# Hybrid decoder block on one core: which stage prepares the stored low parts of the later projection weights

## The chip, the cores and the metric

The kernel runs on one core of a Trainium2 chip. The metric is the device time of one execution in microseconds (us); the median of three runs is given. All data is float32. TensorE computes the matmuls, VectorE (DVE), ScalarE (ACT) and GpSimd (POOL) work between them, and SyncE (SP) issues almost all DMAs. Each engine executes its instructions in the order in which they stand in its queue.

## The reference

One decoder block for a sequence of 1024 tokens with 1024 channels, batch 1. Two branches work on the same normalized input h: attention with 16 heads in stick-breaking form, and a pooling branch.

```python
h = rms_norm(x, norm_gain) * (1 + scale) + shift
q, k, v, z_a, u, z_b, m_a, m_b = split(h @ w_in)          # eight times 1024 columns
p_a = (attention(q, k, v) * silu(z_a)) @ w_branch_a
pooled = (window_mean(u) - u) @ pool_w * pool_scale       # per group of 256 channels, windows 2, 4, 8, 16
p_b = (pooled * silu(z_b)) @ w_branch_b
merged = sigmoid(m_a) * p_a + sigmoid(m_b) * p_b
out = rms_norm(x + gate * (merged @ w_out), final_gain)   # shift, scale, gate = split(silu(c) @ w_ada + b_ada)
```

## The kernel before

**Three matmuls for one.** Every operand of a large product is kept as two tiles: a high part (a cast to a reduced float32 format, `fp32r` in the profile, on ScalarE) and a low part (the operand minus its high part, on VectorE or GpSimd). A product is then high·high + high·low + low·high. So each weight that TensorE uses must first be loaded, cast and subtracted.

**Stages.** In order: the modulation vectors and h (tile `hT`), with the u projection, whose weights are multiplied with `pool_w` first; the *values' stage*, v = h·W_v in two halves of eight tiles (`v{sb}_{hf}`, lines 600 to 627); the *gate's stage*, eight tiles of z_b = h·W (`wzb0` to `wzb7`, lines 662 to 687), each followed by a silu and a multiplication with the pooled differences `d0` to `d7`, written to `gb`; the *products* (lines 750 to 778), p_b = gb·w_branch_b in seven products p1, p5, p6, p7, p4, p3, p2 (a Strassen-Winograd scheme), each with 48 matmuls in two halves q; then 40 weight tiles of *projections* (k, q, z_a and the gates m_a, m_b) with the attention woven in, in a pinned order; then the output.

**The products' banks.** Four banks of PSUM hold the sum of the chain p1, p6, p7, p4. Each of these products adds into what the one before has left there, so ScalarE copies the four banks out in between (`s1` after p1, `s2` after p6, `s3` after p7, `s4` after p4, line 743). The operands of each half are cast into `p1a0`, `p1b0` and so on: the weights (`a`) into two buffers of the pool `wts` (tag `whl`), which the weights of the gate's stage use too; the data (`b`) into three buffers (tag `bhl`).

**Stored low parts.** The order of the 40 projection tiles is in `tiles`. For the first `PLAIN` = 8 of them `load_parts` loads the weight, casts it and subtracts (on GpSimd, tile `MASKED` on VectorE) just ahead of use. For the other 32 the low part is made much earlier, by `make_lo` (lines 147 to 165): load the weight into `l{i}_raw`, cast it into `l{i}_hi` on ScalarE, subtract in place on VectorE, and store the result to `wl_d` in memory; `load_parts` then loads it from there. How many are made where is set by three rows of numbers: eight after the u tiles, `LO_V` after each tile of the values (in each half), `LO_ZB` after each weight of the gate's stage, `LO_PB` after each product. Each call takes buffers from the pool that it is given: three for `l_raw`, one for `l_hi`.

**Buffers.** A tile's buffer is reused when the last reader is done; for `l_raw` this is the store to `wl_d`. In the gate's stage the rows of `w_gate` (`wg0` to `wg7`, the gate vector is summed from them on VectorE, line 686) share the three `lraw` buffers of the pool `pb`. The pool `dif` holds the window sums and differences at the far end of the memory; it is closed after the gate's stage, and `sums` is opened there.

**Order.** The program is written stage by stage, but outside of pinned parts a scheduler puts each engine's queue in order by its own estimate of time. The queues of the built program are shown below where the change moves them.

Of the kernel before, what the change touches and what calls it, by code (L numbers as in the profile page):

```python
# [9 lines left out]
F32 = mybir.dt.float32  # L10
# [5 lines left out]
P = 128  # L16
D = 1024
# [16 lines left out]
NWT = 4  # L34


PLAIN = 8

MASKED = 4
LO_V = (1, 0, 1, 1, 0, 1, 1, 0)  # L40
LO_ZB = (0, 1, 0, 1, 0, 1, 0, 1)
LO_PB = (1, 2, 1, 2, 1, 2, 1)

DIFFS = {1: 0, 4: 1, 7: 2, 10: 3}
HD = 64
# [12 lines left out]
def block_kernel(ctx, tc, a, out):  # L58
# [3 lines left out]
    def pool(name, **kw):  # L62
        return tc.tile_pool(name=name, bufs=1, reuse_waits="tile", **kw)
# [9 lines left out]
    def bank(tag, name):  # L73
        return psp.tile([P, 512], F32, tag=tag, bufs=BANKS[tag], name=name)
# [59 lines left out]
    def load_w(src, name, hi_eng, lo_eng):  # L134
        raw = wts.tile([P, KB, P], F32, tag="raw", bufs=2, name=name + "_raw")
        nc.sync.dma_start(raw.rearrange("p k c -> p (k c)"), src)
        return split(raw, [P, KB, P], wts, "whl", 2, hi_eng, lo_eng, name)
# [6 lines left out]
    tiles += gates  # L144
    early_lo = iter(range(PLAIN, len(tiles)))

    def make_lo(pl, n, bufs=3, later=False):

        rest = []
        for _ in range(n):  # L150
            i = next(early_lo)
            raw = pl.tile([P, D], F32, tag="lraw", bufs=bufs, name=f"l{i}_raw")
            hi = pl.tile([P, D], F32R, tag="lhi", bufs=1, name=f"l{i}_hi")
            nc.sync.dma_start(raw, a["w_in"][tiles[i]])

            def low(i=i, raw=raw, hi=hi):
                act.copy(hi, raw)  # L157
                v.tensor_sub(raw.bitcast(F32R), raw, hi.bitcast(F32))  # L158
                nc.sync.dma_start(wl_d[i], raw)

            if later:
                rest.append(low)
            else:
                low()
        return rest

    def load_parts(i, name):
        if i < PLAIN:
            return load_w(a["w_in"][tiles[i]], name, act, v if i == MASKED else gp)
        raw = wts.tile([P, KB, P], F32, tag="raw", bufs=2, name=name + "_raw")  # L170
        nc.sync.dma_start(raw.rearrange("p k c -> p (k c)"), a["w_in"][tiles[i]])
        hl = wts.tile([P, 2, KB, P], F32R, tag="whl", bufs=2, name=name)
        nc.sync.dma_start(hl[:, 1].rearrange("p k c -> p (k c)").bitcast(F32), wl_d[i])
        act.copy(hl[:, 0], raw)
        return hl[:, 0], hl[:, 1]
# [17 lines left out]
    def project(ct, name, use, he, le):  # L193
        whl = load_w(a["w_in"][ct], name, he, le)
        for sh in range(2):
            ps = any_bank(f"{name}_{sh}")
            mm3(ps, whl, (h_hi, h_lo), range(KB), hmov(sh))
            use(sh, ps)
# [18 lines left out]
    with pool("init") as init:  # L217
# [101 lines left out]
        wg, maps, halves = {}, {}, {}  # L319
# [239 lines left out]
    def load_u(j):  # L559
        u = dif.tile([P, S + 16], F32, tag="u", bufs=2, name=f"u{j}")  # L560
        v.memset(u[:, S:], 0.0)
        nc.sync.dma_start(u[:, :S], u_d[j])
        return u

    def make_d(j, u):
        win = WINDOWS[j // 2]
        cur, n, step = u, S + 16, 1
        while step < win:
            nxt = dif.tile([P, S + 16], F32, tag="win", bufs=2, name=f"win{j}_{step}")
            n -= step  # L570
            v.tensor_add(nxt[:, :n], cur[:, :n], cur[:, step:step + n])
            cur, step = nxt, 2 * step
        t0 = S - win + 1
        d = dif.tile([P, S], F32, tag="d", bufs=5, name=f"d{j}")
        v.scalar_tensor_tensor(d[:, :t0], cur[:, :t0], 1.0 / win, u[:, :t0], ALU.mult, ALU.subtract)
        tl = dif.tile([P, 16], F32, tag="tl", bufs=2, name=f"tl{j}")
        v.tensor_mul(tl[:, :win - 1], cur[:, t0:S], invn[:, 16 - win + 1:])
        v.tensor_sub(d[:, t0:], tl[:, :win - 1], u[:, t0:S])
        dhls[j] = d


    with pool("vp") as vp:
# [17 lines left out]
        for hf in range(2):  # L600
            if hf == 0:
                wv.append([load_wv(1, k2) for k2 in range(4)])
            for sb in range(8):
# [16 lines left out]

                now, todo = todo, make_lo(vp, LO_V[sb], later=True)
                if 8 * hf + sb in DIFFS:
                    j = DIFFS[8 * hf + sb]
# [8 lines left out]
    pb = pbs.enter_context(pool("pb"))  # L632
# [11 lines left out]
    def b_op(src, name):  # L644
        hl = pb.tile([P, 2, 2, 512], F32R, tag="bhl", bufs=3, name=name)
        act.copy(hl[:, 0], src)
        v.tensor_sub(hl[:, 1], src, hl[:, 0].bitcast(F32))
        return hl
# [7 lines left out]
    def a_op(src, name):  # L656
        hl = wts.tile([P, 2, 2, 512], F32R, tag="whl", bufs=2, name=name)
        act.copy(hl[:, 0], src)
        v.tensor_sub(hl[:, 1], src, hl[:, 0].bitcast(F32))
        return hl  # L660

    for j in range(KB):
        if j not in dhls:
            make_d(j, load_u(j))

        def silu(sh, ps):
            z = gb[:, j, sh * 512:sh * 512 + 512]
            act.activation(z, ps, AF.Sigmoid)
            v.tensor_mul(z, ps, z)
            v.scalar_tensor_tensor(z, dhls[j][:, sh * 512:sh * 512 + 512], psc_v[:, j:j + 1], z, ALU.mult, ALU.mult)  # L670

        project(CZB + j, f"wzb{j}", silu, act, v)
        if j < 4:
            v.tensor_sub(t1[:, j], gb[:, j, 512:], gb[:, j, :512])
        else:
            v.tensor_sub(t2[:, j - 4], gb[:, j, 512:], t1[:, j - 4])
            v.tensor_sub(gb[:, j - 4, 512:], gb[:, j, 512:], gb[:, j - 4, 512:])
        make_lo(pb, LO_ZB[j])
        if j == 0:
            nc.sync.dma_start(sg, a["c_row"].broadcast_to([P, D]))  # L680
            gjunk = pb.tile([P, D], F32, tag="lraw", bufs=3, name="gjunk")
            act.activation(gjunk, sg, AF.Sigmoid)
            v.tensor_mul(sg, sg, gjunk)
        wg = pb.tile([P, D], F32, tag="lraw", bufs=3, name=f"wg{j}")
        nc.sync.dma_start(wg, a["w_gate"][j])
        v.scalar_tensor_tensor(wg, wg, 1.0, sg, ALU.mult, ALU.mult, accum_out=gate[:, j:j + 1])
        del dhls[j]
# [4 lines left out]
    sums = pbs.enter_context(pool("sums", side="right"))  # L692
# [45 lines left out]
    def out_b(j, n, t):  # L738
        nc.sync.dma_start(pb_d[j][:, 512 * n:512 * n + 512], t)

    def copied(tag, bufs, j, src):
        t = sums.tile([P, 512], F32, tag=tag, bufs=bufs, name=f"{tag}_{j}")
        act.copy(t, src)
        return t

    def added(t, src):
        v.tensor_add(t, src, t)
        return t

    for n, (name, a_of, b_of) in enumerate(products):  # L750
        c = {"p5": "b", "p3": "b", "p2": "c"}.get(name, "a")
        if c not in chain:
            chain[c] = [bank((tb if c == "b" else ta)[j], f"{name}_{j}") for j in range(4)]
        ps = chain[c]
        for q in range(2):
            wl_, ml_ = a_op(a_of(q), f"{name}a{q}"), b_op(b_of(q), f"{name}b{q}")
            for j in range(4):
                for e in range(2):
                    for i, (w, m) in enumerate(((0, 0), (0, 1), (1, 0))):
                        mm(  # L760
                            ps[j], wl_[:, w, e, j * P:(j + 1) * P], ml_[:, m, e],
                            start=name in ("p1", "p5", "p2") and (q, e, i) == (0, 0, 0), stop=(q, e, i) == (1, 1, 2),
                                skip_group_check=True,
                        )
        for j in range(4):
            if name == "p1":
                keep["s1", j] = copied("s1", 4, j, ps[j])
            elif name == "p6":
                keep["s2", j] = copied("s2", 4, j, ps[j])
            elif name == "p7":  # L770
                out_b(j + 4, 1, added(copied("s3", 2, j, ps[j]), chain["b"][j]))
            elif name == "p4":
                out_b(j + 4, 0, copied("s4", 2, j, ps[j]))
            elif name == "p3":
                out_b(j, 1, added(keep["s2", j], ps[j]))
            elif name == "p2":
                out_b(j, 0, added(keep["s1", j], ps[j]))
        make_lo(pb, LO_PB[n])
    pbs.close()


# [295 lines left out]
    with pool("fin") as fin:  # L1077
# [14 lines left out]
        for sh in range(2):  # L1092
            sl = slice(sh * 512, sh * 512 + 512)
            ms = []
            for j in range(KB):
# [9 lines left out]
                n = 0  # L1105
# [12 lines left out]
            for i in range(4):  # L1118
# [8 lines left out]
                for c_, cl in enumerate(pieces):  # L1127
                    w_ = cl.stop - cl.start
                    ps = bank(("z", "tr")[c_ % 2], f"o{sb}_{c_}")[:, :w_]
                    n = 0  # L1130
# [85 lines left out]
```

## Time and profile before

| | us |
|---|---|
| median of 3 runs | 1216.52 (1215.63 to 1218.12) |
| profiled execution | 1219.61 |
| its span, first to last instruction | 1217.9 |
| TensorE busy, matmuls | 1194.0 (98%) |
| VectorE busy | 796.7 (65%) |
| ScalarE busy | 549.9 (45%) |
| GpSimd busy | 167.9 (14%) |

| stage | from, us | to, us |
|---|---|---|
| values | 128.4 | 215.5 |
| gate's stage | 215.5 | 305.1 |
| products | 310.1 | 396.9 |
| projections with attention | 396.9 | 1036 |

The granted clock of TensorE is 0.995 of full speed over the span. In lists of instructions a row gives start, duration, engine, line, operation, output and inputs by the program's names, shapes and count; in brackets stands how long the engine was idle before, and who ended that. Numbers of buffers are left out of names, and so `p` stands both for the tiles of the products and for those of the projections, and `l_raw` for all of `l8_raw` to `l39_raw`.

### The profile page before, as it was taken

The numbers are of one execution on the slowest core, as the hardware profiler recorded it, in microseconds if no ns is written. First come the engines' busy times: TensorE is split into PE (matmuls) and PEld (weight loads), VectorE is DVE, ScalarE is ACT, GpSimd is POOL, SyncE is SP. The second block draws the span as 40 slices with busy tenths as digits, with TensorE's granted clock in tenths as the row PEclk, the third lists the DMA queues.
The fourth block names the chain that finished last, engine by engine and source line by source line (L and its number), as shares of the span: only waits on it lengthen the run. The fifth ranks groups of instructions, "written<-read, shape, count | busy, mean of one in ns | idle before, by whom it ended". The sixth has DMA issues, their size and how long they took to land.

```text
span 1217.9 us, 16134 instructions
## 1 busy us (share of the span) xinstructions
PE 1194.0 (98%) x5698; PEld 995.8 (82%) x5698; DVE 796.7 (65%) x1088; ACT 549.9 (45%) x1020; POOL 167.9 (14%) x352
## 2 busy tenths in 40 slices
PE   8999999999699999999999999999999999999997
PEld 7888888887488888888888888888888888888886
DVE  5754591686675186777768678687777753795643
ACT  5564331332453255655656555555655653232211
POOL 1000000000000333222222221222221210000001
PEclk9999999999899999999999999999999999999999
DMA  9649994767735732343534325353353335985622
GB/s 350 259 168 360 308 380 169 231 221 166 271 138 178 224 92 70 107 135 104 162 116 138 101 95 164 110 155 99 110 143 100 96 123 173 352 273 168 208 72 84
DMA packets 85699, 212.39 MB, mean 174 GB/s; under 512 B 10609, under 2 KB 24049, under 8 KB 83442
## 3 DMA queue, kind: packets, MB, share of 16 engines
q1 hardware_dynamic: 77410, 196.47, 49.8%
q10 hardware_dynamic: 8208, 14.88, 3.3%
q8 instruction: 45, 0.74, 0.3%
q14 instruction: 36, 0.29, 0.1%
HBM read 144.20 MB, written 50.34 MB: 160 GB/s over the span
## 4 chain that ended last, share of the span: by engine, by line
PE 82%; DMA 7%; DVE 5%; issue 4%; ACT 1%; POOL 0%; SPq 0%; POOLq 0%; ACTq 0%; DVEq 0%
PE p L108 38%; PE v L108 7%; PE o L108 6%; PE z L108 6%; PE av L108 5%; PE wt L108 5%; PE pa L108 5%; PE u L108 4%; DMA wl_d<-l_raw 3%; PE ua L108 3%; DMA l_raw<-in_w_in 1%; PE wm L108 1%; DMA m<-sb_d 1%; PE wzb L108 1%; DMA kh<-kh 1%
## 5 line engine op out<-in xcount | busy, mean ns | idle before, releaser
L108 PE MATMUL p<-hT,w 128*128 128x512 f32 x1920 | 480.1, 391 | 0.6 <-ACT m_sg L203 0.6
L108 PEld LDWEIGHTS p<-hT,w 128*128 128x128 f32 x1920 | 355.2, 188 | 74.8 <-ACT m_sg L203 1.0
L938 DVE TENSOR_TENSOR_SCAN om<-om 128x512 f32<-128x512 f32 (+7 forms) x128 | 175.7, 1373 | 124.7 <-ACT om L931 69.1
L931 ACT ACTIVATE om<-z 128x512 f32<-128x512 f32 (+2 forms) x192 | 94.5, 492 | 156.4 <-PE z L108 133.9
L957 ACT CAST wt<-wt 128x512 fp32r<-128x512 f32 (+1 forms) x160 | 88.2, 551 | 48.2 <-PE wt L108 47.9
L958 DVE TENSOR_TENSOR wt<-wt,wt 128x512 fp32r<-128x512 f32 (+1 forms) x160 | 99.2, 620 | 16.2 <-ACT wt L957 15.6
L108 PE MATMUL av<-wt,vv 128*128 128x512 f32 x320 | 106.4, 414 | 0.0
L936 POOL TENSOR_SCALAR_AFFINE_SELECT om<-om 128x128 f32<-128x128 f32 x128 | 56.4, 441 | 346.9 <-ACT om L931 287.5
L108 DVE TENSOR_TENSOR be<-be,om 128x511 f32<-128x511 f32 (+7 forms) x128 | 95.1, 748 | 1.1 <-POOL be L936 0.7
L932 ACT ACTIVATE be<-z 128x512 f32<-128x512 f32 (+2 forms) x192 | 94.1, 490 | 0.0
L108 PE MATMUL pa<-ga,wa 128*128 128x512 f32 x384 | 89.9, 390 | 0.7 <-DVE s L1110 0.6
L108 PE MATMUL o<-wo,mhl 128*128 128x512 f32 (+1 forms) x408 | 89.6, 377 | 0.0
L108 PE MATMUL wzb<-hT,wzb 128*128 128x512 f32 x384 | 87.6, 390 | 2.0 <-DVE wzb L123 2.0
L108 PE MATMUL wt<-ident,be 128*128 128x128 f32 x576 | 89.4, 273 | 0.0
L108 PE MATMUL v<-wv,hT 128*128 128x512 f32 x384 | 87.2, 389 | 0.0
L108 PEld LDWEIGHTS wzb<-hT,wzb 128*128 128x128 f32 x384 | 71.9, 188 | 17.5 <-DVE wzb L123 2.5
L108 PEld LDWEIGHTS pa<-ga,wa 128*128 128x128 f32 x384 | 71.9, 188 | 16.4 <-issue 1.0
L108 PEld LDWEIGHTS o<-wo,mhl 128*128 128x128 f32 x408 | 73.5, 188 | 14.1
L108 PEld LDWEIGHTS v<-wv,hT 128*128 128x128 f32 x384 | 72.1, 188 | 14.9
L108 PEld LDWEIGHTS wt<-ident,be 128*128 128x128 f32 x576 | 70.2, 141 | 11.6
L157 ACT CAST l_hi<-l_raw 128x1024 fp32r<-128x1024 f32 x32 | 33.6, 1051 | 72.6 <-DMA l_raw<-in_w_in 54.8
L158 DVE TENSOR_TENSOR l_raw<-l_raw,l_hi 128x1024 fp32r<-128x1024 f32 x32 | 39.1, 1222 | 41.7 <-ACT l_hi L157 41.6
(175 smaller groups left out, 1481.8 us busy)
## 6 DMA issues: line engine op xcount, KB each, us to landing
w_raw<-in_w_in SPq DMA_DIRECT2D x40, 512.0 KB, 4.6
l_raw<-in_w_in SPq DMA_DIRECT2D x32, 512.0 KB, 4.9
wl_d<-l_raw SPq DMA_DIRECT2D x32, 512.0 KB, 5.9
w<-wl_d SPq DMA_DIRECT2D x32, 512.0 KB, 4.0
v_d<-vo SPq DMA_DIRECT2D x16, 512.0 KB, 5.2
vv<-v_d SPq DMA_DIRECT2D x8, 1024.0 KB, 5.3
wa_raw<-in_w_branch_a SPq DMA_DIRECT2D x16, 512.0 KB, 4.8
wa<-in_w_mod SPq DMA_DIRECT2D x7, 1024.0 KB, 6.3
```

Of the source, the lines that this page charges most:

```text
L108: ins = op(*args, **kw)
L157: act.copy(hi, raw)
L158: v.tensor_sub(raw.bitcast(F32R), raw, hi.bitcast(F32))
L931: act.activation(om[:, b0:b0 + n], zp[:, :n], AF.Sigmoid, scale=-0.125)
L932: act.activation(be[:, b0:b0 + n], zp[:, :n], AF.Sigmoid, scale=0.125)
L936: gp.affine_select(out=tl[:, :P], in_=tl[:, :P], pattern=[[1, P]], compare_op=ALU.is_gt, fill=fill, base=0, channel_multiplier=-1)
L938: v.tensor_tensor_scan(om[:, :W], om[:, :W], om[:, :W], 1.0, ALU.mult, ALU.min)
L957: act.copy(wt[:, 0, :off], pt[:, :off])
L958: v.tensor_sub(wt[:, 1, :off], pt[:, :off], wt[:, 0, :off].bitcast(F32))
```

## The change

Four numbers change, and where three tiles live. `PLAIN` goes from 8 to 10, so 30 low parts are stored, and the projection tiles 8 and 9 (`w_8`, `w_9`) are subtracted on GpSimd. `LO_V` goes from five to seven per half, 14 in the values' stage in place of 10. `LO_ZB` and its call are gone. `LO_PB` gives eight in place of ten, and these now take two `l_raw` buffers and one `l_hi` buffer from `sums`, whose place the window sums and differences had, and not from `pb`. `wg` and `gjunk` have one buffer of their own in place of the three shared ones. The numbers of the l's move by two: what was `l25` before stands as `l27` now.

```diff
-PLAIN = 8
+PLAIN = 10
...
-LO_V = (1, 0, 1, 1, 0, 1, 1, 0)
-LO_ZB = (0, 1, 0, 1, 0, 1, 0, 1)
-LO_PB = (1, 2, 1, 2, 1, 2, 1)
+LO_V = (1, 1, 1, 1, 1, 1, 1, 0)
+LO_PB = (0, 2, 1, 2, 1, 1, 1)
...
-        make_lo(pb, LO_ZB[j])
         if j == 0:
             nc.sync.dma_start(sg, a["c_row"].broadcast_to([P, D]))
-            gjunk = pb.tile([P, D], F32, tag="lraw", bufs=3, name="gjunk")
+            gjunk = pb.tile([P, D], F32, tag="wg", bufs=1, name="gjunk")
...
-        wg = pb.tile([P, D], F32, tag="lraw", bufs=3, name=f"wg{j}")
+        wg = pb.tile([P, D], F32, tag="wg", bufs=1, name=f"wg{j}")
...
-        make_lo(pb, LO_PB[n])
+        make_lo(sums, LO_PB[n], 2)
```

**SP's queue at the end of the gate's stage.** `wzb7_raw` is the last weight of that stage, `g_d` the gate vector's store, `a11_0` and `a11_1` are the two halves of p1's weight, `a21`, `a22` and `a11s` go into p5 and p6; `l{i}_raw<-in_w_in` is a load for a low part and `wl_d<-l{i}_raw` its store. Before:

```order
L136 DMA wzb7_raw_2272<-in_w_in 128x1024
L689 DMA g_d_74<-gate_1728 128x8x1
L159 DMA wl_d_79<-l30_raw_2427 128x1024
L154 DMA l33_raw_2593<-in_w_in 128x1024
L159 DMA wl_d_79<-l31_raw_2513 128x1024
L154 DMA l34_raw_2685<-in_w_in 128x1024
L653 DMA a11_0_2355<-in_w_branch_b 128x2x512
L159 DMA wl_d_79<-l32_raw_2519 128x1024
L154 DMA l35_raw_2691<-in_w_in 128x1024
L159 DMA wl_d_79<-l33_raw_2593 128x1024
L653 DMA a11_1_2387<-in_w_branch_b 128x2x512
```

Of the change:

```order
L135 DMA wzb7_raw_2278<-in_w_in 128x1024
L687 DMA g_d_74<-gate_1752 128x8x1
L652 DMA a11_0_2355<-in_w_branch_b 128x2x512
L652 DMA a11_1_2387<-in_w_branch_b 128x2x512
L652 DMA a21_0_2431<-in_w_branch_b 128x2x512
L652 DMA a22_0_2433<-in_w_branch_b 128x2x512
L652 DMA a11s_0_2436<-in_w_branch_b 128x2x512
L153 DMA l32_raw_2507<-in_w_in 128x1024
L652 DMA a21_1_2469<-in_w_branch_b 128x2x512
L153 DMA l33_raw_2513<-in_w_in 128x1024
```

The loads and stores of low parts that stood ahead of p1's weights are gone, and the first load of one now stands behind the weights of p1 and half of p5's. ScalarE's casts `l_hi` and VectorE's subtractions moved in the same way.

**VectorE's queue between the second and the fourth weight of the gate's stage.** `wg2` and `wg3` are the reads of w_gate's rows, `wzb3` is the low part of the fourth weight; the others are pooling sums (`win`), silus (`gb`) and the low part of p1's first data half (`p1b0`). Of the change:

```order
L684 SCALAR_TENSOR_TENSOR wg2_1952,gate_1752<-wg2_1952,sg_1755 128x1024
L570 TENSOR_TENSOR win6_2_2185<-win6_1_2183 128x1037
L560 MEMSET u7_2262 128x16
L669 SCALAR_TENSOR_TENSOR gb_1749<-d1_1374,vecs_89,gb_1749 128x512
L570 TENSOR_TENSOR win6_4_2187<-win6_2_2185 128x1033
L684 SCALAR_TENSOR_TENSOR wg3_2017,gate_1752<-wg3_2017,sg_1755 128x1024
L646 TENSOR_TENSOR p1b0_2360<-gb_1749,p1b0_2360 128x1024
L570 TENSOR_TENSOR win6_8_2189<-win6_4_2187 128x1025
L668 TENSOR_TENSOR gb_1749<-wzb1_1_1858,gb_1749 128x512
L122 TENSOR_TENSOR wzb3_1957<-wzb3_raw_1955,wzb3_1957 128x1024
```

Before, `wg2` and `wg3` stood ahead of `wzb3` too, with two low parts (`l26`, `l27`) between them, and `wg1` stood behind `wzb2`; now `wg1` stands ahead of it. With one buffer the load of each `wg` waits for the read of the one before.

**ScalarE's queue between p6 and p4.** `s2_0` to `s2_3` are the copies of the banks after p6, `s3_0` and so on those after p7; `p7a1`, `p4b0` and the like are casts of operands. Before:

```order
L743 COPY s2_0_2585<-p1_0_2351 128x512
L743 COPY s2_1_2587<-p1_1_2352 128x512
L743 COPY s2_2_2589<-p1_2_2353 128x512
L743 COPY s2_3_2591<-p1_3_2354 128x512
L658 CAST p7a1_2639<-a11d_1_2634 128x1024
L646 CAST p4b0_2703<-t2_1727 128x1024
L658 CAST p4a0_2699<-a22_0_2697 128x1024
L646 CAST p4b1_2736<-t2_1727 128x1024
L743 COPY s3_0_2669<-p1_0_2351 128x512
```

Of the change:

```order
L741 COPY s2_0_2579<-p1_0_2351 128x512
L741 COPY s2_1_2581<-p1_1_2352 128x512
L156 CAST l36_hi_2686<-l36_raw_2685 128x1024
L741 COPY s2_2_2583<-p1_2_2353 128x512
L741 COPY s2_3_2585<-p1_3_2354 128x512
L657 CAST p7a1_2633<-a11d_1_2628 128x1024
L645 CAST p4b0_2697<-t2_1751 128x1024
L156 CAST l37_hi_2770<-l37_raw_2769 128x1024
L657 CAST p4a0_2693<-a22_0_2691 128x1024
L645 CAST p4b1_2730<-t2_1751 128x1024
L156 CAST l38_hi_2850<-l38_raw_2849 128x1024
L741 COPY s3_0_2663<-p1_0_2351 128x512
```

Three casts of low parts' weights, l36, l37 and l38, now stand among the copies; `l39` follows ahead of `s3_2`. On TensorE the products keep their order, except that p5's second half starts with two matmuls per bank, then two per bank of p6 follow, and then the rest of p5.

## The prediction

> **What bounds the kernel now.** I read the waits of TensorE first, then its timeline, then the granted clock by stretch, then the queues. TensorE is busy 98% of the span, so only its few pauses can be won. The view of the waits (engine and tile, line, who was waited for: us in total, times, longest) puts nearly all of them at two places, the gate's stage (wzb, z_b = h·W) and the start of the products (tiles p1 to p7):
> ```profile
> PE p L108 <- ACT p1a L658: 8.5, 2, 4.9
> PE wzb L108 <- DVE wzb L123: 2.0, 1, 2.0
> PE p L108 <- ACT p5a L658: 1.7, 1, 1.7
> ```
> TensorE's timeline (start, us, operation, count, idle before) shows them in order:
> ```profile
> 215.48 76.87 PE L108 MATMUL wzb<-hT,wzb 128*128 128x512 f32 x338
> 294.38 10.73 PE L108 MATMUL wzb<-hT,wzb 128*128 128x512 f32 x46 [2.04 <-DVE wzb L123]
> 310.05 1.22 PE L108 MATMUL p<-p1b,p1a 128*128 128x512 f32 x2 [4.94 <-ACT p1a L658]
> 311.61 6.71 PE L108 MATMUL p<-p1b,p1a 128*128 128x512 f32 x22 [0.34 <-DVE p1a L659]
> 321.88 7.22 PE L108 MATMUL p<-p1b,p1a 128*128 128x512 f32 x24 [3.56 <-ACT p1a L658]
> 330.85 11.28 PE L108 MATMUL p<-p5b,p5a 128*128 128x512 f32 x48 [1.74 <-ACT p5a L658]
> ...
> 341.97 11.15 PE L108 MATMUL p<-p6b,p6a 128*128 128x512 f32 x48
> 352.95 11.15 PE L108 MATMUL p<-p7b,p7a 128*128 128x512 f32 x48
> ...
> 396.90 23.33 PE L108 MATMUL p<-hT,w 128*128 128x512 f32 x102
> ```
> Undisturbed, a matmul costs 76.87 / 338 = 0.2274 us, and a product of 48 takes 352.95 - 341.97 = 10.98. So eight gate weights (384 matmuls, 87.3 us) and p1 need 98.3 us, but from 215.48 to p5 at 330.85 they took 115.4. **17.1 us are lost there**, more than the pauses: the matmuls of p1 are slow as well. The clock says why (stretch, then busy time by engine, then granted clock, DMA share, GB/s):
> ```profile
> 290.00:305.00 15.00, 12.96 (x56) 10.00 (x55) 9.74 (x12) 4.15 (x6) 0.00 (x0) 1.00 0.75 221
> 312.00:314.00 2.00, 2.00 (x6) 1.52 (x6) 1.60 (x4) 1.16 (x2) 0.00 (x0) 0.50 1.02 371
> 321.80:324.00 2.20, 2.12 (x5) 1.73 (x6) 2.20 (x3) 0.98 (x2) 0.00 (x0) 0.50 0.58 238
> ```
> After pauses of 4.94 and 3.56 us the clock is 0.50; after the pause of 2.04 us it stays 1.00. Each slow spell costs about 2.1 us: the 24 matmuls from 310.05 end at 318.32, 8.27 - 0.34 - 5.46 = 2.5 too many, the next 24 take 7.22 - 5.46 = 1.8.
>
> Who is late? ScalarE, with p1a; and it had stood waiting for an l (the raw weight whose low part is made), placed ahead of p1a in its queue; the l waited in SP's queue for an earlier l's store:
> ```profile
> 307.52 1.04 ACT L157 CAST l_hi<-l_raw 128x1024 fp32r<-128x1024 f32 x1 [4.96 <-DMA l_raw<-in_w_in]
> 308.48 0.59 ACT L668 ACTIVATE gb<-wzb 128x512 f32<-128x512 f32 x1
> 308.96 1.03 ACT L658 CAST p1a<-a 128x1024 fp32r<-128x1024 f32 x1
> ...
> SPq L154 <- DMA wl_d<-l_raw: 61.8, 17, 12.0
> ```
>
> **The change, part by part.** *The l's leave the gate's stage.* Before, 14 stood there in SP's, ScalarE's and VectorE's order (four by LO_ZB, ten of LO_PB pulled ahead). Now none does: SP issues a11_0 right behind the gate's store. p1a's first half needs the weight buffer of wzb6, free at 291.9; its second half that of wzb7, free at 302.8 = 215.48 + 87.3, and then takes a silu of 0.59, a cast of 1.03 and, on VectorE, two 512-wide operations and a low part, to about 306, against the 308.3 at which it is wanted. p1 starts at 302.8 without a pause: **minus 17.1** if nothing new is late.
>
> *Four more l's with the values.* The rows up to the first tile of the second half stand as they did; the four more fall behind it, between the copies of the values:
> ```profile
> 128.00:172.00 44.00, 44.00 (x196) 36.45 (x195) 32.83 (x47) 14.71 (x18) 0.00 (x0) 1.00 0.98 344
> 172.00:216.00 44.00, 44.00 (x196) 36.45 (x195) 16.13 (x21) 9.03 (x13) 0.00 (x0) 1.00 0.58 215
> ```
> There VectorE (second after TensorE's two columns) has 28 of 44 us free and ScalarE 35; 4 x (1.23 + 1.05) fits, and 4 MB of DMA raise 215 GB/s to 306, under the 344 before it. Eight banks of PSUM lie between a late copy and TensorE. Cost 0; without that cover, 4 x 2.28 = 9.1.
>
> *One buffer for w_gate.* wg had three buffers; now each load waits until VectorE has read the one before, and VectorE stands at the wg, with the next weight's low part queued behind it, for which TensorE waits. Per round: landing and a read.
> ```profile
> 222.47 0.75 DVE L670 SCALAR_TENSOR_TENSOR gb<-d,vecs,gb 128x512 f32<-128x512 f32 x1
> ...
> DMA to landing us min/median/max: 3.4/4.7/6.1
> ...
> L686 DVE SCALAR_TENSOR_TENSOR wg<-wg,sg x8: 1211/1218/1225, 225.6 to 262.0; 128x1024 f32<-128x1024 f32 x8
> ...
> 338.03 1.22 DVE L722 TENSOR_TENSOR t<-gb,t 128x1024 f32<-128x1024 f32 x1
> 339.17 1.22 DVE L713 TENSOR_TENSOR a11d<-a11d,a21d 128x1024 f32<-128x1024 f32 x1
> ```
> (The second row is wg's landing times; the last two start 1.14 apart, which is what an operation costs in a row.) VectorE is done with the first silu at 223.2, so the first read can end at 224.4, if sg, now issued ahead of the last value's store, is there. Three rounds of 4.7 + 1.2 with the operations between them put wzb3's low part at 246.4; it is wanted at 248.6, three weights of 10.91 and two matmuls behind 215.48. Likewise wzb4's comes at 257.7 (wanted 259.5) and wzb5's at 268.0 (270.5). So the cost is 0 with about 2 us to spare, and a first read that starts as late as before, at 225.6, just uses them up. At a landing of 6.1 the three come at 250.6, 264.7 and 277.8: pauses of 2.0, 3.2 and 2.1, together 7.3. I take 0, the end that the median row gives, and keep both.
>
> *Eight l's among the products.* This is the new danger. They have two buffers, so every second load waits for a store, and their casts stand in ScalarE's queue ahead of the copies s2 and s3, which must be taken before the next product adds into the same banks of PSUM. A round is store, load, cast, low part.
> ```profile
> wl_d<-l_raw SPq DMA_DIRECT2D x6, 512.0 KB, 4.8
> ...
> a<-in_w_branch_b SPq DMA_DIRECT2D x5, 512.0 KB, 4.2
> ...
> 305.00:331.00 26.00, 15.42 (x50) 11.27 (x50) 16.81 (x19) 10.91 (x14) 0.00 (x0) 0.80 0.75 278
> 331.00:364.00 33.00, 33.00 (x145) 26.99 (x146) 23.83 (x22) 16.16 (x20) 0.00 (x0) 1.00 0.42 144
> ...
> 350.41 0.59 ACT L743 COPY s<-p 128x512 f32<-128x512 f32 x1 [0.75 <-PE p L108]
> ```
> The first row is the median store from 300 to 400 us, the second the median load of the same size from 325 to 400. With 19 transfers of 0.5 MB between 313 and 350 the traffic is about 260 GB/s, nearer to the 278 of 305 to 331 than to the 144 of the stretch behind it, so I take 4.8 and 4.2. The walk: p1 ends at 313.8; p6b's low part waits for its buffer, the last copy (0.6) and its cast (1.0), 315.4; from it to l34's low part VectorE has ten operations of 1.14 and then l34's own, so l34 is ready at 327.9. Store, 332.8; load of l36, 337.0; cast, 338.1; copies s2_2 and s2_3 to 339.1. p7 wants the bank of s2_2 at 302.8 + 3 x 10.98 + 12 x 0.2274 = 338.5, and gets it at 338.6: 0.1. l36's low part 339.3; store 344.1; load of l38 348.4; cast 349.4; s3_0 350.1. p4 wants that bank at 302.8 + 4 x 10.98 = 346.7: **a pause of 3.4 us**. It is next to the 3.56 after which the clock fell, so I add 2.1; the slow spell hides that p4a's second low part is ready only at 354. l39's cast (354.6) and s3_2 (355.2) come before their bank's turn. Sum: 0.1 + 3.4 + 2.1 = **plus 5.6**; ends 0 and 16.6 (below).
>
> *Two weights not stored.* Tiles 8 and 9 make their low part on GpSimd again, 2.39 us each, in among the selects of the attention:
> ```profile
> 484.69 2.39 POOL L123 TENSOR_TENSOR w<-w_raw,w 128x1024 fp32r<-128x1024 f32 x1
> ...
> 498.83 1.06 ACT L174 CAST w<-w_raw 128x1024 fp32r<-128x1024 f32 x1
> ...
> 515.59 1.05 ACT L174 CAST w<-w_raw 128x1024 fp32r<-128x1024 f32 x1
> ```
> One more tile starts each 16.8 us, so the low part is ready some 12 us early, and the selects behind it come up to 2.4 us late, as behind the row at 484.69, after which TensorE did not pause. Cost 0, at most 2 x 2.4 = 4.8 without that slack. Two loads and two stores less save nothing by themselves.
>
> **Sum.** The profiled execution took 1219.61 us with a span of 1217.9; minus 17.1 plus 5.6 is minus 11.5: span 1206.4, execution 1208.1. The median of the runs, 1216.52, lies 3.1 below that execution, so **1205.0 us**.
>
> **The rivals.** *Quick rounds* (1199.4 us). If a store lands as the values' stores did and a load as a12s did, 3.1 + 3.6:
> ```profile
> v_d<-vo SPq DMA_DIRECT2D x8, 512.0 KB, 3.1
> ...
> a12s<-in_w_branch_b SPq DMA_DIRECT2D x2, 512.0 KB, 3.6
> ```
> then l38's cast ends at 344.8, before p7's first bank is finished, and the whole 17.1 stay: 1216.5 - 17.1. For it: the queue holds less. Against: these rows are from quiet stretches. The Trainium skill's rule for a lone transfer ("DMA: Bandwidth & Descriptors", Anatomy of one DMA), 2.0 us plus bytes over 436 GB/s, gives an estimate of 3.2 us for 0.5 MB; it is stated for the other issuing path, and the busy rows exceed it.
>
> *The clock stays* (1202.9 us). The pause of 3.4 lies between 2.04, which left the clock alone, and 3.56, which did not; without the slow spell 2.1 less is lost. For it: the pause may come out shorter. Against: 3.56 is the nearer row. The Trainium skill ("TensorE: Matmul & The Clock Gate", Part 1) has the clock halve after a whole idle window of about 3.4 us, whose phase runs freely. The two rows agree with that, and by it a pause of 3.4 could go either way.
>
> *wg late* (1212.3 us). The 7.3 above on top of the forecast, from a landing of about 5.1 us on, where the spare time is spent. Against: fewer transfers beside it than the rows had.
>
> *Late selects* (1209.8 us): the 4.8 above on top.
>
> *Slow rounds, slower than before* (1219.0 us). At the landings of the values' first half,
> ```profile
> wl_d<-l_raw SPq DMA_DIRECT2D x9, 512.0 KB, 6.9
> ...
> l_raw<-in_w_in SPq DMA_DIRECT2D x8, 512.0 KB, 7.2
> ```
> the same walk gives s2_2 at 345.0 (pause 6.5) and s3_0 at 361.2 (pause 5.9), each with a slow spell of 2.1: 16.6, nearly all that is won. Each further us of store and load adds 3, since three rounds (l32, l34, l36) lie ahead of l38; from 15.1 us together it is slower by over 0.2%: 1216.5 - 17.1 + 19.6 = 1219.0. Against it: the DMA share was 0.98 there, and even that gives 14.1.
>
> *Nothing changes* (1216.5 us): the loads of the branch weights remain behind something. Against: the order.
>
> **How the numbers follow.** Forecast 0.36, quick rounds 0.26, the clock stays 0.15, wg late 0.11, late selects 0.04, slow rounds 0.05, nothing 0.03. About 0.2%, 2.4 us, is what a measurement of this kernel can tell from no change. Faster is the first five, 0.92; same 0.03; slower 0.05. The range 1198.5 to 1211.0 reaches from all 17.1 won (with 0.9, the lowest run below the median) to the forecast with most of wg's price, and leaves out the rest.
>
> **What would show it.** Right: no pause at p1, clock 1.00 from 290 to 345, p1 start near 302.8, one pause of 2 to 4 us at the first matmul of p4 with ScalarE's s3 as releaser and an l's load ahead of it. Wrong: pauses at wzb3 to wzb5 released by VectorE (wg), at p7 (l36), or among the projections near the two GpSimd rows; or p1 still waiting for p1a.

## The result and the profile after

The changed kernel takes 1206.48 us in the median of 5 runs (1205.32 to 1210.55) beside 1216.31 of the kernel before (1215.63 to 1218.12): a ratio of 0.9926, with a 95% interval of 0.9905 to 0.9947. That is 9.8 us less, where 11.5 were forecast. The profiled execution is the slowest of the five, 1210.55 us with a span of 1208.8.

TensorE's waits after the change (the same view as before):

```profile
PE p L107 <- ACT s L741: 3.0, 1, 3.0
PE p L107 <- DVE klo L107: 2.3, 1, 2.3
...
PE wt L107 <- DVE wt L956: 0.4, 1, 0.4
```

Nothing waits for p1a or wzb any more. Two waits are left that are worth a look: one for ScalarE's copies `s`, and one that stood nowhere before, for `klo`, the low part of the first projection. TensorE's timeline shows where they lie:

```profile
128.06 87.20 PE L107 MATMUL v<-wv,hT 128*128 128x512 f32 x384
215.10 87.20 PE L107 MATMUL wzb<-hT,wzb 128*128 128x512 f32 x384
302.14 11.17 PE L107 MATMUL p<-p1b,p1a 128*128 128x512 f32 x48
313.14 7.62 PE L107 MATMUL p<-p5b,p5a 128*128 128x512 f32 x32
...
335.54 11.49 PE L107 MATMUL p<-p7b,p7a 128*128 128x512 f32 x48
349.99 12.75 PE L107 MATMUL p<-p4b,p4a 128*128 128x512 f32 x48 [2.96 <-ACT s L741]
...
384.57 11.07 PE L107 MATMUL p<-hT,w 128*128 128x512 f32 x48
397.94 14.58 PE L107 MATMUL p<-hT,w 128*128 128x512 f32 x63 [2.30 <-DVE klo L107]
412.36 0.39 PE L107 MATMUL z<-kh,q 128*128 128x512 f32 x1
```

The values and the gate's stage run as one unbroken row of 384 matmuls each, and p1 starts at 302.14 without a pause. Then comes a pause of 2.96 ahead of p4, and p4 itself takes 12.75 in place of 11.15. The last pause, 2.30, lies behind the products.

The last row, the first matmul of the attention's scores, is a good end for a comparison. Before, it stood here:

```profile
422.47 0.47 PE L108 MATMUL z<-kh,q 128*128 128x512 f32 x1 [0.20 <-DMA q<-qlo]
```

The stretch from the start of the gate's stage to this row I call **the stretch**. It leaves out what varies ahead of it (the gate's stage began between 214.8 and 217.7 in the profiles below) and the attention behind it. It took 422.47 - 215.48 = 206.99 before and 412.36 - 215.10 = 197.26 after: 9.73 less, about the 9.8 of the medians. (The spans of the two profiled executions differ by 9.1.) So the result lies in it, in three parts:

| from one profile each, us | before | after | difference |
|---|---|---|---|
| gate's stage and p1, to the start of p5 | 115.37 | 98.04 | -17.33 |
| p5 to the end of p2 | 66.05 | 71.43 | +5.38 |
| end of p2 to the first score matmul | 25.57 | 27.79 | +2.22 |

Each is the difference of two starts in the timeline (the end of p2 is the start of the row behind it). The first two were forecast, the third was not.

**The third part.** ScalarE's and SP's timelines of the changed kernel (start, us, operation, in brackets the idle time before and who ended it; on SP the row is the issue):

```profile
396.58 1.07 ACT L824 CAST kh<-p 128x512 fp32r<-128x512 f32 x2 [10.75 <-DMA pb_d<-s]
...
384.53 0.98 SPq L839 DMA_DIRECT2D vv<-v_d x2
385.61 0.62 SPq L737 DMA_DIRECT2D pb_d<-s x1
```

The cast of the first `kh` waits 10.75 us, and not for its matmuls but for a store of `s`. In the built program the first `kh` buffer lies where three of the four copies `s1` lay: `sums` has grown by three buffers for the l's, and this pushed `s1` down into the place that `kh` gets when `sums` is closed. The last `s1` is stored at 385.61, behind two loads of 1 MB; it lands 10.9 us after its issue, and the cast begins at once. The late store is not new: before the change the last `s1`, issued at 397.99 behind the same two loads, landed after 9.9 us, and nothing waited for it. There the cast followed its matmuls:

```profile
402.59 0.59 ACT L826 CAST kh<-p 128x512 fp32r<-128x512 f32 x1 [4.44 <-PE p L108]
```

### The profile page after: what moved, and what is told of

Same layout as the page of the kernel before. It is cut to its first block, busy times and chain, and to the rows that moved or that the text cites. A ratio compares the mean times of both kernels' runs of the same rounds, so it can differ in the third digit from the quotient of the medians.

```text
span 1208.8 us, 16123 instructions
## 1 busy us (share of the span) xinstructions
PE 1192.3 (99%) x5698; PEld 994.8 (82%) x5698; DVE 796.9 (66%) x1086; ACT 548.1 (45%) x1018; POOL 172.1 (14%) x354
## 4 chain that ended last, share of the span: by engine, by line
PE 86%; DMA 4%; issue 4%; DVE 4%; ACT 1%; POOL 0%; SPq 0%; POOLq 0%; ACTq 0%; DVEq 0%
PE p L107 37%; PE wzb L107 7%; PE v L107 7%; PE o L107 6%; PE z L107 5%; PE av L107 5%; PE wt L107 5%; PE pa L107 5%; PE u L107 5%; PE ua L107 3%; PE wm L107 1%; DMA m<-sb_d 1%; DMA pb_d<-s 1%; DMA l_raw<-in_w_in 1%; DMA wl_d<-l_raw 1%
## 5 line engine op out<-in xcount | busy, mean ns | idle before, releaser
L122 POOL TENSOR_TENSOR w<-w_raw,w 128x1024 fp32r<-128x1024 f32 x9 | 22.2, 2466 | 350.0 <-ACT w L127 350.0
L107 PE MATMUL z<-kl,q 128*128 128x512 f32 (+2 forms) x192 | 65.5, 341 | 0.0
```

The lines of the kernel that those rows point to most:

```text
L107: ins = op(*args, **kw)
L122: lo_eng.tensor_tensor(lo, src, hi.bitcast(F32), op=ALU.subtract)
```

## The experiments

All are variants of the changed kernel or of the kernel before. Medians, and ratios to the kernel before as run beside them (1216.78, 1220.09 and 1218.51 us in the three sets of runs: experiments 1 to 4, 5 to 8, and 9). The last column is the stretch in the profiled execution.

| | l's in gate's stage / products / not stored | median, us (range) | ratio, 95% interval | stretch, us |
|---|---|---|---|---|
| before | 4 and ten pulled in / - / 8 | 1216.31 (1215.63 to 1218.12) | 1 | 206.99 |
| changed | 0 / 8 / 10 | 1206.48 (1205.32 to 1210.55) | 0.9926, 0.9905 to 0.9947 | 197.26 |
| 1 s1 elsewhere | 0 / 8 / 10 | 1207.12 (1206.04 to 1207.21) | 0.9915, 0.9898 to 0.9931 | 195.65 |
| 2 six between | 0 / 6 / 12 | 1203.74 (1203.30 to 1206.47) | 0.9893, 0.9874 to 0.9913 | 191.95 |
| 3 both | 0 / 6 / 12 | 1202.77 (1202.36 to 1203.66) | 0.9882, 0.9865 to 0.9898 | 190.30 |
| 4 none between | 0 / 0 / 18 | 1201.95 (1201.15 to 1202.56) | 0.9875, 0.9855 to 0.9895 | 189.32 |
| 5 changed again | 0 / 8 / 10 | 1208.22 (1206.74 to 1210.22) | 0.9907, 0.9889 to 0.9925 | 195.97 |
| 6 before, no gate lows | ten pulled in / - / 12 | 1205.78 (1204.47 to 1207.44) | 0.9887, 0.9870 to 0.9903 | 194.15 |
| 7 before, no product lows | 4 / 0 / 18 | 1202.07 (1201.46 to 1204.17) | 0.9859, 0.9842 to 0.9875 | 189.24 |
| 8 all late | 0 / 0 / 32 | 1203.67 (1202.32 to 1204.34) | 0.9865, 0.9848 to 0.9882 | 189.63 |
| 9 three buffers | 0 / 8 / 10 | 1206.15 (1204.82 to 1209.87) | 0.9898, 0.9882 to 0.9914 | 193.27 |

**Experiment 1: s1 in another place.** Is the overlap with `kh` the cause of the pause at klo?

```diff
     s2k = sums.tile([P, 4, 512], F32, name="s2k")
+    for tag, bufs, shape, dt in (
+        ("ar", 2, [P, 2, 512], F32), ("lraw", 2, [P, D], F32), ("lhi", 1, [P, D], F32R),
+        ("s2", 4, [P, 512], F32), ("s3", 2, [P, 512], F32), ("s4", 2, [P, 512], F32),
+    ):
+        sums.tile(shape, dt, tag=tag, bufs=bufs, name=f"{tag}_place")
```

> The changed kernel with the copies s1 laid elsewhere: other buffers of the same pool are given their places ahead of s1, so that s1 no longer lies under the buffer of the first kh. Nothing is left out; the order of the instructions is the same. Theory (kh waits until the last s1 has been stored, and the pause of 2.30 us before the sums of klo comes from it): the 10.75 us wait of ScalarE at the cast of kh goes, the pause of 2.30 goes, time 2.3 us below the changed kernel, some 1204.2. Rival (the buffer of kh has other late owners, or the store lands late for whatever lies there): the pause stays between 1.5 and 2.3, time within 0.5 of the changed kernel.

TensorE's and ScalarE's timelines of this kernel (its lines stand five lower in the file, so L741 is L746 here):

```profile
349.79 13.78 PE L107 MATMUL p<-p4b,p4a 128*128 128x512 f32 x48 [3.33 <-ACT s L746]
...
385.41 25.33 PE L107 MATMUL p<-hT,w 128*128 128x512 f32 x111
...
391.06 0.59 ACT L829 CAST kh<-p 128x512 fp32r<-128x512 f32 x1 [4.40 <-PE p L107]
```

The mechanism is shown: the cast of kh now follows its matmuls, and the 111 matmuls from 385.41 run without a pause. The last store of `s1` still lands late, after 10.1 us, but nothing waits for it. The time did not follow: 1207.12 lies inside the runs of the changed kernel (the ratio is 0.0011, or 1.3 us, lower, with intervals that overlap). The pause and the slow clock at p4 cost 3.33 + (13.78 - 11.15) = 5.96 here, against 2.96 + 1.60 = 4.56 in the first profile of the changed kernel, and that took back 1.4 of the 2.3. The longer spell comes from where the pause lay among the steps in which the clock is set (last section): here the clock fell 1.4 us before the pause ended and stayed low for 6.83 us, there 0.2 before its end and for 3.41. The price of the pause at klo shows better in experiment 3.

**Experiment 2: six l's among the products.** `l38` and `l39` leave; two more weights get their low part on GpSimd.

```diff
-PLAIN = 10
+PLAIN = 12
...
-LO_PB = (0, 2, 1, 2, 1, 1, 1)
+LO_PB = (0, 2, 1, 2, 1, 0, 0)
```

> The changed kernel with six l's among the products in place of eight; the two left out there (l38 and l39) join the weights that are not stored and are made by GpSimd in the projection, 12 in place of 10. Nothing of the computation is left out. Theory (p4 waits because ScalarE casts l38 only when its load has landed, and the copies s3 stand behind that cast): the pause of 2.96 before p4 goes, and the slow clock behind it with about 1.6, time 4 to 4.6 us below the changed kernel, some 1202.2; the pause at klo stays. Rival (two more weights without a stored low cost GpSimd and VectorE time in the projection that the matmuls wait for, up to 2.4 each): the pause at p4 goes but the projection ends as much later, time 1206 to 1207.

```profile
346.00 3.83 PE L107 MATMUL p<-p4b,p4a 128*128 128x512 f32 x16
350.81 7.60 PE L107 MATMUL p<-p4b,p4a 128*128 128x512 f32 x32 [0.97 <-DVE p4a L658]
...
392.52 14.57 PE L107 MATMUL p<-hT,w 128*128 128x512 f32 x63 [1.21 <-DVE klo L107]
```

p4 starts at 346.00, right behind p7; ScalarE is no longer waited for. Something that the pause had covered shows instead: the low part of p4a's second half, late by 0.97. The stretch is 5.3 shorter than in the first profile of the changed kernel and 4.0 shorter than in its second (experiment 5). Expected were 4 to 4.6: the medians give 2.7 (1206.48 to 1203.74), the ratios, each to the kernel before beside it, 0.0033 or 4.0.

**Experiment 3: both.** The two edits above in one kernel.

> Both edits of the two runs before in one kernel: s1 laid elsewhere and six l's among the products. Nothing is left out. Theory (the two pauses are apart, one at p4 and one at klo, and their costs add): 6.3 to 6.9 us below the changed kernel, some 1199.9. Rival (they do not add: with p4 earlier the vv loads and the store meet differently, or something next in line, such as the first weight wt, is late instead): no more than 5 below, 1201.5 or above.

```profile
350.56 7.60 PE L107 MATMUL p<-p4b,p4a 128*128 128x512 f32 x32 [0.64 <-DVE p4a L658]
...
379.98 25.33 PE L107 MATMUL p<-hT,w 128*128 128x512 f32 x111
```

1202.77 us. Here the pause at klo costs what it shows. Against experiment 2 the klo pause of 1.21 is gone, the wait for p4a is 0.64 in place of 0.97, the stretch is 1.65 shorter and the median 0.97 lower. Against the changed kernel 6.3 to 6.9 were expected: the stretch is 7.0 and 5.7 shorter than in its two profiles, the ratio gives 5.4 (0.0044), the medians 3.7. The profiled executions of the changed kernel were slower than its median, so the two pauses are probably worth somewhat less in an ordinary run. In the stretch their costs add, as the theory has it; the median lies in the rival's range (1201.5 or above), but of the rival's way there, something next in line that is late instead, only the 0.64 for p4a shows.

**Experiment 4: none among the products.**

```diff
-PLAIN = 10
+PLAIN = 18
...
-LO_PB = (0, 2, 1, 2, 1, 1, 1)
+LO_PB = (0,) * 7
```

> The changed kernel with no l at all among the products: the eight join the weights that are not stored, 18 in place of 10, made by GpSimd in the projection. Nothing of the computation is left out. Theory (the late lows are made beside the matmuls and cost nothing): the same as six between, some 1202.2, pause at klo unchanged. Rival (each late low above some number is waited for, up to 2.4 us each): 8 more lows give up to 19 us, time anywhere from 1204 to 1225.

```profile
301.95 11.17 PE L107 MATMUL p<-p1b,p1a 128*128 128x512 f32 x48
...
345.91 11.15 PE L107 MATMUL p<-p4b,p4a 128*128 128x512 f32 x48
...
378.87 25.37 PE L107 MATMUL p<-hT,w 128*128 128x512 f32 x111
```

From 215 to 404 there is no pause at all. The pause at klo is gone as well, which was not expected: without the l's, `sums` is as small as before, and `kh` lies clear of `s1`. 1201.95 us; eight more late low parts cost nothing that shows.

**Experiment 5: the changed kernel again,** to see whether the two pauses belong to it or to one execution.

> The changed kernel once more, unaltered, for a second profile of it beside the other runs of this call. Theory (the 2.30 us before the sums of klo and the 2.96 before p4 belong to the kernel): both pauses are there again, klo at 1.5 to 3, p4 at 2.5 to 3.5; time 1205.3 to 1207.5. Rival (they belong to the slowest of the first five executions, 1210.55 us, which was the profiled one): one of them is under 0.5 and the span is some 1204.

```profile
349.18 12.86 PE L107 MATMUL p<-p4b,p4a 128*128 128x512 f32 x48 [3.10 <-ACT s L741]
...
396.43 14.59 PE L107 MATMUL p<-hT,w 128*128 128x512 f32 x63 [1.47 <-DVE klo L107]
```

Both are there, 3.10 and 1.47. The one at p4 is stable, the one at klo moves with the landing of the store: 10.9 us and a pause of 2.30 in the first profile, 10.0 and 1.47 here, 9.7 and 1.21 in experiment 2. (For the cast of `kh` the profile names TensorE here; but the cast begins at 395.06, just as the store issued at 384.96 lands, 11.2 us behind the first of its matmuls, where experiment 1 needs 5.65.) The median, 1208.22, is 0.7 above the range that was given; the kernel before ran 3.8 slower in this set of runs too, so a median is best set against the kernel before of its own set, as the ratios do.

**Experiment 6: the kernel before without the four l's of LO_ZB.** Which of its l's made p1 late?

```diff
-PLAIN = 8
+PLAIN = 12
...
-LO_ZB = (0, 1, 0, 1, 0, 1, 0, 1)
+LO_ZB = (0,) * 8
```

> The kernel before without LO_ZB's four l's in the gate's stage; 12 weights in place of 8 are not stored and are made by GpSimd in the projection. LO_PB's ten stay in the pool of the gate's stage, with three buffers, and still stand ahead of the loads of p1 in SP's queue. Nothing is left out. Theory (p1 waits because the ten of LO_PB are pulled ahead of its operands): p1 still waits for p1a, the pauses in all shrink only in part, time 1209 to 1214. Rival (the four of LO_ZB crowd the gate's stage): the pauses at wzb and p1 go, time 1199 to 1202.

```profile
303.30 0.74 PE L108 MATMUL p<-p1b,p1a 128*128 128x512 f32 x2 [1.26 <-ACT p1a L658]
305.65 12.39 PE L108 MATMUL p<-p1b,p1a 128*128 128x512 f32 x46 [1.62 <-DVE p1a L659]
...
300.76 1.05 ACT L157 CAST l_hi<-l_raw 128x1024 fp32r<-128x1024 f32 x1 [2.30 <-DMA l_raw<-in_w_in]
...
302.21 1.04 ACT L658 CAST p1a<-a 128x1024 fp32r<-128x1024 f32 x1
```

p1 waits for p1a as before, with the cast of an l ahead of it in ScalarE's queue, but less of the loss is left than my theory had: 1205.78 lies between its 1209 to 1214 and the rival's 1199 to 1202. The stretch is 12.8 shorter than before, and 4.9 above that of experiment 7. Four l's fewer in the chain through the three buffers are worth 12.8 / 4 = 3.2 us each, slow clock included; p1 itself starts 6.1 earlier, counted from the start of the gate's stage. So the four are part of the loss as long as the ten are there. Fourteen rounds don't fit into the gate's stage, ten nearly do (4.9 lost), and four do (experiment 7).

**Experiment 7: the kernel before without LO_PB's ten.**

```diff
-PLAIN = 8
+PLAIN = 18
...
-LO_PB = (1, 2, 1, 2, 1, 2, 1)
+LO_PB = (0,) * 7
```

> The kernel before without LO_PB's ten l's; 18 weights in place of 8 are not stored. LO_ZB's four stay in the gate's stage, and wg shares the three buffers with them as before. Nothing is left out. Theory (the ten pulled ahead are the cause of the whole loss): no wait for p1a, a pause of at most 0.5 at wzb, time 1199 to 1201. Rival (the four of LO_ZB are part of it): a pause stays in the gate's stage with a slow clock behind it, time 1203 to 1212.

```profile
214.86 87.20 PE L108 MATMUL wzb<-hT,wzb 128*128 128x512 f32 x384
301.90 11.17 PE L108 MATMUL p<-p1b,p1a 128*128 128x512 f32 x48
```

The whole loss is gone with LO_ZB's four still in the gate's stage and wg still in the shared buffers: a stretch of 189.24, 17.75 less than before, and a ratio of 0.9859. The median of 1202.07 is over the 1199 to 1201 expected; the kernel before took 1220.09 beside it, and 17.75 less is 1202.3. Of the change's parts, this one (the ten leave the gate's stage) is enough; the rest of the change is not needed for it. Taking them out empties both the queues and the three buffers, so which of the two held p1 up is not told apart here.

**Experiment 8: 32 low parts late.** How far does "GpSimd makes it for nothing" carry?

```diff
-PLAIN = 10
+PLAIN = 32
...
-LO_V = (1, 1, 1, 1, 1, 1, 1, 0)
-LO_PB = (0, 2, 1, 2, 1, 1, 1)
+LO_V = (0,) * 8
+LO_PB = (0,) * 7
```

> The changed kernel with no l in the values' stage and none among the products: LO_V and LO_PB are all zero, only the eight l's of the u stage are stored, and 32 of the 40 projection weights are not stored, so GpSimd makes their low part just ahead of use. Nothing is left out. Theory (a late low lies beside the matmuls: GpSimd has a whole weight's time, some 16 us, for 2.4 us of work): time 1201.5 to 1202.5, as with 18 late. Rival (the late lows push VectorE's selects, and from some number the matmuls wait): 14 more lows give up to 2.4 each, 1205 to 1235.

```profile
PE wt L107 <- DVE wt L956: 1.4, 3, 0.5
```

1203.67, 1.6 above experiment 7 in the same set of runs (0.7 by the ratios), for 14 more: some 0.1 us each, and not 2.4. The forecast of 1201.5 to 1202.5 was too low by 1.2. This one wait has grown from 0.4 to 1.4. The rest of the 1.6 I can't place, as the ranges overlap; part of it need not belong to the low parts, for in the two profiled executions the values' stage began 0.87 us later than in experiment 7 (128.69 and 127.82), ahead of anything in which the two differ.

**Experiment 9: a third buffer for the l's.** Do the two buffers set the pause at p4, as the walk in the prediction has it?

```diff
-                out_b(j + 4, 0, copied("s4", 2, j, ps[j]))
+                out_b(j + 4, 0, copied("s3", 2, j, ps[j]))
...
-        make_lo(sums, LO_PB[n], 2)
+        make_lo(sums, LO_PB[n], 3)
```

> The changed kernel with three buffers for the l's among the products in place of two; for their room the copies s4 share the two buffers of s3. Eight l's stay there and nothing is left out. Theory (a round of two l's through two buffers, load, cast and store, sets when l38 can be cast, and so p4's pause): l38 and l39 are loaded a round earlier, no pause of over 1 at p4 and no slow clock behind it, time 3.5 to 5 below the changed kernel, some 1202 to 1204 beside its 1206.5 to 1208.2. Rival (SP's queue and its traffic set it, not the buffers: eight loads and eight stores of 0.5 MB stand between the products' own): ScalarE still waits for the l's, at p4 or, as the casts now stand earlier, at p6 or p7, and 3 us or more are lost there; time 1206 or above.

```profile
323.50 2.12 PE L107 MATMUL p<-p5b,p5a 128*128 128x512 f32 x8 [2.08 <-ACT p5a L657]
...
351.10 11.36 PE L107 MATMUL p<-p4b,p4a 128*128 128x512 f32 x48
...
319.92 1.05 ACT L156 CAST l_hi<-l_raw 128x1024 fp32r<-128x1024 f32 x1 [1.48 <-DVE l_raw L157]
...
322.41 1.04 ACT L657 CAST p5a<-a 128x1024 fp32r<-128x1024 f32 x1
```

Both theories were partly right. With a third buffer the pause at p4 is gone and no slow clock follows, so the two buffers did set it. But the casts of the l's now stand earlier: two in a row, of which the second waits 1.48 for VectorE to free the only `l_hi`, and p5a's second half is cast behind them. TensorE pauses 2.08 there. The stretch is 193.27, 4.0 and 2.7 shorter than in the two profiles of the changed kernel; in the medians (1206.15, ratio 0.9898) it can't be told from it.

## Why the prediction was nearly right

**The l's leave the gate's stage (-17.1): right, -17.33.** p1 starts at 302.14 (forecast 302.8) without a pause. Experiments 6 and 7 support the reason: rounds of load, cast, low part and store through shared buffers, ahead of p1a. What the prediction did not see is that not all of it had to go: the second half of p1 started 13.6 us late (321.88, where 308.3 was wanted), and without the ten of LO_PB the four that stay cost nothing.

**Four more l's with the values (0): right.** 384 matmuls in 87.20, one row.

**One buffer for w_gate (0, at most 7.3): right.** The view of the tile `wg` gives the landing of its loads, and how long VectorE stood idle for them:

```profile
DMA wg<-in_w_gate: 1.6, 2
...
DMA to landing us min/median/max: 3.3/3.5/4.4
```

The landings are shorter than the 4.7 taken from before, probably because the l's no longer load beside them (not tried alone), and VectorE's two waits of 1.6 together reached no matmul.

**Eight l's among the products (+5.6): right in place, +5.38 in size, and in part by luck.** The walk had l36's cast done at 338.1, l38's at 349.4, s3_0 at 350.1. ScalarE's timeline:

```profile
336.91 1.05 ACT L156 CAST l_hi<-l_raw 128x1024 fp32r<-128x1024 f32 x1 [2.46 <-DMA l_raw<-in_w_in]
337.87 1.06 ACT L741 COPY s<-p 128x512 f32<-128x512 f32 x2
...
348.40 1.04 ACT L156 CAST l_hi<-l_raw 128x1024 fp32r<-128x1024 f32 x1 [3.59 <-DMA l_raw<-in_w_in]
349.35 1.07 ACT L741 COPY s<-p 128x512 f32<-128x512 f32 x2
```

338.0, 349.4, and s3_0 some 0.53 (half of the two copies) behind 349.35. The store and load taken from the busier rows (4.8 and 4.2) were the right choice: the DMA view from 300 to 350 us (the last number is the median landing) has:

```profile
l_raw<-in_w_in SPq DMA_DIRECT2D x7, 512.0 KB, 4.4
wl_d<-l_raw SPq DMA_DIRECT2D x6, 512.0 KB, 5.0
```

The pause is 2.96 in place of 3.4, as p4 was wanted at 347.0, and the slow clock behind it cost 1.6 where 2.1 was taken: 4.56 in place of 5.5. Most of the rest of the 5.38 is nothing that the prediction saw. From the start of p5 to the end of p7 TensorE took 33.89 us in this profile without a pause, and 33.15 in the second profile of the same kernel (experiment 5); p5's first 32 matmuls started 0.233 us apart here and 0.229 there. In the second profile the pause and the slow clock cost 4.81 and the three parts are -17.33, +4.92 and +1.39, so 11.0 us less in all. Experiment 2 takes two l's out and the pause goes; experiment 9 adds a buffer and it goes.

**Two weights not stored (0): right,** and experiments 4 and 8 carry it to 18 and nearly to 32.

**What failed: there was no term for the place that `sums` takes.** The prediction ended its sum with p2 and had nothing in it for the three new buffers of `sums`. They moved `s1` onto the first `kh`, and a store that nothing had waited for became a wait of 10.75 us on ScalarE and of 2.30 (1.47 in the second profile) on TensorE. This is the 2.2 of the third part. Up to the end of p2 the stretch came out 0.5 better than the 11.5 forecast, and behind it 2.2 worse: 9.7 in place of 11.5. That is the 1.5 us by which the median lies above 1205.0, as the kernel before came out 0.2 faster too (1216.31 in place of 1216.52). In the set of experiment 5 the ratio of 0.9907 gives 11.3 less.

**The rivals.** *The clock stays* fell: the clock halved after 2.96, 3.10 and 3.33 us alike (below). *Quick rounds* fell with the landings of 5.0 and 4.4. *wg late*, *late selects*, *slow rounds* and *nothing changes* did not come. Of the signs of being right one reads differently: the clock from 290 to 345 is 0.95 in the first profile, as it is nearly everywhere in it, and 1.00 in the second.

The two pauses on which the forecast of the slow clock rested, of 2.04 and 3.56 us, were told apart by their length. The traces show that length alone doesn't decide it: what counted is how the pause lay among steps of 3.41 us (last section). That the clock fell at p4 was right; that 2.1 would be its price was an average of spells of one step and of two.

**A better version.** Experiments 4 (ratio 0.9875) and 7 (0.9859) are faster than the kernel before by 1.25% and 1.4%, each with an interval that ends below 0.99; their medians, 1201.95 and 1202.07, lie 4.5 and 6.2 below the changed kernel's (1206.48 in its own set, with the kernel before at 1216.31 there and 1216.78 beside experiment 4; 1208.22 beside experiment 7). The interval of experiment 4 doesn't touch that of the changed kernel's first set, nor that of experiment 7 the one of experiment 5. Experiment 7 changes two lines of the kernel before.

## What to carry to other kernels

Before work is moved into a stage that has room for it, ask whether it has to be done ahead at all: here 18 low parts were made just ahead of use (17 of them on GpSimd, which was busy 16% of the time with them) at no cost that shows, while ten more l's in the gate's stage and eight among the products each cost a pause. The stages with room to spare bore theirs: 14 l's with the values, and four in the gate's stage. A pool that grows moves what lies beside it: look at which later tile gets its place, and which store, behind which loads, that tile must then wait for. And where a rotation of few buffers feeds casts into an in-order queue, walk it in time against the copies behind them; this walk was right to under a microsecond, while the medians could not tell experiments 1 and 9 from the changed kernel.

## What the runs showed of the hardware

**The clock falls after less than 3 us of idle time, and it changes only at steps of 3.41 us.** TensorE in the changed kernel, the pause of 2.96 ending at 349.99 (stretch, busy time, granted clock, DMA share, GB/s):

```profile
348.00:350.00 2.00, 0.01 (x1) 0.90 0.65 243
350.00:352.00 2.00, 2.00 (x5) 0.50 0.74 227
352.00:354.00 2.00, 2.00 (x8) 0.68 0.94 376
354.00:356.00 2.00, 2.00 (x11) 0.95 0.74 243
```

And in experiment 6, after pauses of 1.26 and 1.62 with two matmuls (0.74) between them:

```profile
306.00:308.00 2.00, 2.00 (x6) 0.50 0.56 154
308.00:310.00 2.00, 2.00 (x8) 0.73 0.89 275
```

A pause of 2.04 in the kernel before, one of 2.08 in experiment 9 and the one of 2.30 at klo in the changed kernel left it alone. So the length of a pause alone does not decide. The trace records when the granted clock changes (us from the span's start; the last column is worked out from it and TensorE's rows):

| profile | pause of TensorE | clock falls | rises | idle in the 3.41 us ahead of the fall |
|---|---|---|---|---|
| before | 305.11 to 310.05 | 307.84 | 314.66 | 2.73 |
| before | 318.32 to 321.88 | 321.49 | 324.90 | 3.17 |
| changed | 347.03 to 349.99 | 349.76 | 353.18 | 2.74 |
| experiment 1 | 346.46 to 349.79 | 348.43 | 355.25 | 1.96 |
| experiment 5 | 346.08 to 349.18 | 349.98 | 353.39 | 2.61 |
| experiment 6 | 302.04 to 305.65, with 0.74 of work in it | 305.66 | 309.08 | 2.67 |

Each low spell lasts 3.41 or 6.83 us, and in the kernel before, which has two, all four changes lie 3.41 us or twice that apart. So the clock is set at steps of 3.41 us that run on through the execution, and a fall can come in a pause or, as in experiment 5, 0.8 us behind it. Cut into such steps, the eleven profiles agree on a limit: every step at full clock with 1.96 us or more of idle time ended in a fall, and none with 1.91 or less did. (The ends of matmuls are modelled in a profile, so this holds to about a tenth of a microsecond.) The pause of 2.30 at klo was spared because a step ended in it: 1.91 lay ahead of the end and 0.39 behind. In the changed kernel the step behind the fall held 0.2 us of idle time and the clock rose again; in experiment 1 it held 1.4, and the clock stayed low for a second step.

The Trainium skill ("TensorE: Matmul & The Clock Gate", Part 1) puts the fall behind a whole idle window of about 3.4 us, whose phase runs freely. The steps of 3.41 agree with its window; but here about 2 us of idle time in one were enough, even with matmuls in between, so the measurement decides. The cost varied from 1.60 to 2.63 us of p4 for pauses of 2.96 to 3.33.

**The recorded clock of a whole execution can be low at next to no cost.** In the first profile of the changed kernel it is 0.947 over the span and 0.95 where nothing disturbs TensorE, but 384 matmuls took the same 87.20 us as in experiment 7 with 1.00. It is not quite free: p5 to p7 took 0.74 us longer than in experiment 5, and 32 matmuls of the first 25 us (`wm`, 128x256) 7.36 in place of the 7.07 of experiment 4. Why some rows show it and others don't stays open.

**A small store issued behind large loads landed late.** The DMA view of the changed kernel from 380 to 396 us:

```profile
vv<-v_d SPq DMA_DIRECT2D x2, 1024.0 KB, 8.9
pb_d<-s SPq DMA_DIRECT2D x4, 256.0 KB, 4.8
```

The four stores are of one size and went through one queue; the last, right behind the two loads, landed 10.9 us after its issue, more than twice the median. The same store took 9.9 us in the kernel before and in experiment 4, 10.1 in experiment 1, 10.0 in experiment 5, and 9.7 in experiments 2 and 9. That the loads ahead of it are the reason was not tried apart.
